# Splitting a mixture-of-experts layer's weights five chunks ahead instead of three

## The chip, the cores and the metric

The kernel runs on one core of a Trainium2 chip. The metric is the device time in microseconds of one execution. Before the change the median of 3 runs is 1571.48 us (1569.36 to 1572.67).

## The reference

The reference computes one decoder layer on 512 tokens of width 1024, in float32: an RMS norm with a shift and scale from a conditioning vector, an input projection, retention and differential attention side by side, an output projection, and then a feed-forward part with 32 experts, of which each token uses 4. A final RMS norm closes it. Cut to what matters here:

```python
logits = xt @ w_router + b_router
top_v, top_i = lax.top_k(logits, 4)          # 4 of 32 experts for each token
gate = softmax(top_v)
# for each expert e and its tokens xb:
hid = xb @ w1[e] + b1[e]                     # w1[e]: 1024 x 2048
y = swiglu_clamped(hid) @ w2[e] + b2[e]      # w2[e]: 1024 x 1024
out[token] += gate * y
```

## The kernel before

All 32 experts are run one after the other, each on up to 128 of its tokens. Almost all weights of the program are those of the experts: for each expert w1 comes in 8 chunks of 128 x 2048 numbers and w2 in 4 chunks of the same size, 1 MB each. That makes 12 chunks for an expert and 384 in all.

The products are made in float32 precision out of a faster format (fp32r) that keeps fewer bits. Each operand is split into a high half, which is its rounded value, and a low half, which is the rest. Three products are added: high x high (L521), high x low of the weights (L522), and low of the tokens x high (L523). A chunk of weights is therefore split first: ACT makes the high half (L481), and DVE subtracts it from the raw chunk in place (L484); POOL does L484 for a few chunks around the first expert. One chunk is 12 products on PE: 4 each of L521, L522 and L523.

Weights live in 48 pages of 4 KB for each partition, and one chunk fills two pages. A raw chunk takes one pair of pages, a split chunk two pairs, because its low half stands where the raw chunk was. `Whole(n)` (a kind of `Conv`) is the reserve of split chunks: `run` splits on until `ahead` = n chunks are held, counting the one that PE is using. `Stream.pump` issues the transfers of the next raw chunks on SP's queue as soon as pages are free, but leaves 2 pages for each split that is still to be made:

```python
kept = self.keep
if self.conv is not None:
    kept += 2 * (self.conv.ahead - len(self.conv.made))
if self.mem.n_free - n < kept or self.mem.find(n) is None:
    return
```

When PE has used up a chunk, `Whole.done` frees its four pages, the next raw chunk is sent for, and the next split is made. In the expert part 12 pages or so are held by other buffers, so that 18 pairs are left for weights: 3 split chunks and 12 raw ones before. From `e == E - LAST - 1` on, `st.keep = 12` holds 12 pages back for the sums at the end.

The loop over the experts runs w1 of expert e (16 calls of `w1_unit`) and then w2 of expert e - 1 (8 calls of `w2_unit`), so that what lies between the two products has time. Around them stand small steps on all engines: `index` finds the tokens of an expert two ahead (L1064 to L1080; the gather is an indirect DMA on POOL), `turn` and `turn_hidden` transpose tokens on PE (L1092, L1099) and split them on ACT and DVE (L1087, L1088), `w1_start` puts the bias into PSUM (L1109), `swiglu` runs on ACT and DVE (L1127 to L1129), and `result` scales the output (L1205, ACT) and adds it into a table in DRAM (L1206, POOL). In the tail the table is read back and added (L1176, L1177, DVE), and the last two experts are put in by products (L1160).

The source is not the order in which the instructions run. A scheduling layer takes the program when it is built and fixes, for each engine, the order in which its instructions stand, by its own estimates of how long things take. On the chip each engine then works through its list from the top, and an instruction that waits holds up all behind it. So a number such as the depth of the reserve moves instructions in all lists.

Of the kernel before, what the change touches and what calls it, by code (L numbers as in the profile page):

```python
# [191 lines left out]
def decoder_layer(ctx, tc, t, out):  # L192
# [793 lines left out]
                      OH[:, i, :].bitcast(F32), start=(i == 0 and k % 4 == 0), stop=(i == NT - 1 and k % 4 == 3))  # L986
            tc.keep_in_program_order(ins)

    cm = Whole(3)
    u1, u2 = {}, {}  # L990
    for e in range(E + 1):
        if e < E:
# [487 lines left out]
```

## Time and profile before

| | us |
|---|---|
| median of 3 runs | 1571.48 |
| profiled execution | 1568.56 |
| its span | 1566.6 |
| PE busy | 1468.6 |
| DVE busy | 1319.4 |
| ACT busy | 1002.4 |
| POOL busy | 164.1 |

The expert part fills the span from about 320 us on. The shares are averages over the whole span. A PE that is shown as busy is not a PE at its peak, because the ends of its instructions are modelled and overlap by some 0.17 us; what a stretch costs is better read from the distance between instructions that come once for each expert. All times below are from the start of the span.

### The profile page before, as it was taken

The numbers are of one execution on the slowest core, as the hardware profiler recorded it, in microseconds if no ns is written. First come the engines' busy times: TensorE is split into PE (matmuls) and PEld (weight loads), VectorE is DVE, ScalarE is ACT, GpSimd is POOL, SyncE is SP. The second block draws the span as 40 slices with busy tenths as digits, with TensorE's granted clock in tenths as the row PEclk, the third lists the DMA queues.
The fourth block names the chain that finished last, engine by engine and source line by source line (L and its number), as shares of the span: only waits on it lengthen the run. The fifth ranks groups of instructions, "written<-read, shape, count | busy, mean of one in ns | idle before, by whom it ended". The sixth has DMA issues, their size and how long they took to land.

```text
span 1566.6 us, 18635 instructions
## 1 busy us (share of the span) xinstructions
PE 1468.6 (94%) x6837; PEld 1193.5 (76%) x6837; DVE 1319.4 (84%) x1407; ACT 1002.4 (64%) x917; POOL 164.1 (10%) x92
## 2 busy tenths in 40 slices
PE   3999999788999999999999999999999999999976
PEld 3787678666888888888887777777777777887754
DVE  6868767977999899899988888888888888888886
ACT  4435434465777777777767666666666666776753
POOL 0000000422100110000011000000000001110001
PEclk8999999988999999999999999999999999999978
DMA  9871473658999999999999999999999999997862
GB/s 371 319 271 37 153 269 138 252 201 320 354 359 367 364 355 362 367 368 365 371 360 349 347 341 346 340 346 345 345 342 335 343 351 345 353 344 259 310 228 98
DMA packets 88812, 485.19 MB, mean 310 GB/s; under 512 B 12433, under 2 KB 18996, under 8 KB 39182
## 3 DMA queue, kind: packets, MB, share of 16 engines
q1 hardware_dynamic: 75792, 453.54, 77.2%
q0 software_dynamic: 9360, 18.05, 4.7%
q10 hardware_dynamic: 3566, 12.37, 2.1%
q8 instruction: 56, 0.92, 0.2%
q14 instruction: 38, 0.31, 0.1%
HBM read 475.82 MB, written 25.44 MB: 320 GB/s over the span
## 4 chain that ended last, share of the span: by engine, by line
PE 74%; DVE 12%; DMA 7%; ACT 5%; issue 2%; POOL 0%; ACTq 0%; DVEq 0%; SPq 0%; POOLq 0%
PE ps L522 22%; PE ps L523 22%; PE ps L521 20%; DVE part L484 6%; DMA page<-in_w_dram 5%; ACT part L481 4%; PE ps L1099 2%; PE ps L1109 1%; PE ps L1092 1%; DVE page L372 1%; PE ps L708 1%; PE ps L788 1%; PE ps L797 1%; PE ps L733 1%; DMA page<-x_dram 0%
## 5 line engine op out<-in xcount | busy, mean ns | idle before, releaser
L484 DVE TENSOR_TENSOR part<-page,part 128x2048 fp32r<-128x2048 f32 x380 | 861.4, 2290 | 106.2 <-ACT part L481 104.2
L481 ACT ACTIVATE part<-page 128x2048 fp32r<-128x2048 f32 x384 | 726.2, 1914 | 144.5 <-PE ps L522 133.3
L522 PE MATMUL ps<-part,part 128*128 128x512 f32 x1792 | 718.9, 401 | 33.1 <-DVE part L484 28.2
L523 PE MATMUL ps<-part,part 128*128 128x512 f32 x1792 | 706.3, 394 | 3.4 <-DVE part L1088 3.4
L521 PE MATMUL ps<-part,part 128*128 128x512 f32 x1792 | 634.0, 397 | 5.7 <-ACT part L616 3.2
L522 PEld LDWEIGHTS ps<-part,part 128*128 128x128 f32 x1792 | 339.6, 189 | 118.1 <-DVE part L484 45.7
L521 PEld LDWEIGHTS ps<-part,part 128*128 128x128 f32 x1792 | 339.5, 190 | 80.8 <-issue 3.7
L523 PEld LDWEIGHTS ps<-part,part 128*128 128x128 f32 x1792 | 339.4, 189 | 73.5 <-DVE part L1088 4.1
L1087 ACT ACTIVATE part<-ps 128x512 fp32r<-128x512 f32 x128 | 73.8, 598 | 139.7 <-PE ps L522 64.8
L1206 POOL DMA_INDIRECT y_dram<-page,idx x30 | 74.8, 2492 | 771.1 <-ACT page L1205 735.7
L1088 DVE TENSOR_TENSOR part<-ps,part 128x512 fp32r<-128x512 f32 x128 | 86.4, 686 | 33.3 <-ACT part L1087 33.2
L1127 ACT ACTIVATE page<-ps 128x512 f32<-128x512 f32 x64 | 37.4, 586 | 74.0 <-PE ps L523 74.0
L1080 POOL DMA_INDIRECT page<-h_dram,idx x31 | 46.4, 1497 | 246.1 <-DVE gs L1071 232.8
L1128 DVE TENSOR_SCALAR page<-ps 128x512 f32<-128x512 f32 x64 | 43.8, 687 | 10.8 <-ACT page L1127 10.8
L447 ACT ACTIVATE part<-page 128x1024 fp32r<-128x1024 f32 x32 | 33.5, 1055 | 27.3 <-DMA page<-in_w_in_dram 9.0
L1129 DVE SCALAR_TENSOR_TENSOR page<-page,page 128x512 f32<-128x512 f32 x64 | 46.7, 733 | 0.0
L450 DVE TENSOR_TENSOR part<-page,part 128x1024 fp32r<-128x1024 f32 x32 | 38.7, 1221 | 9.2 <-ACT part L447 8.9
L1099 PEld LDWEIGHTS ps<-ident,page 128*128 128x128 f32 x256 | 40.1, 203 | 7.1 <-issue 2.5
L420 DVE SCALAR_TENSOR_TENSOR page<-page,sc,page 128x1024 f32<-128x1024 f32 x32 | 40.9, 1280 | 4.6 <-DMA page<-in_w_ada_dram 4.1
L1109 PE MATMUL ps<-part,selr 128*128 128x512 f32 x128 | 39.4, 403 | 4.7 <-DVE page L1128 3.8
L1099 PE MATMUL ps<-ident,page 128*128 128x128 f32 x256 | 41.8, 284 | 2.1 <-DVE page L1129 2.1
L1092 PE MATMUL ps<-ident,page 128*128 128x128 f32 x248 | 37.4, 272 | 0.0
(219 smaller groups left out, 774.2 us busy)
## 6 DMA issues: line engine op xcount, KB each, us to landing
page<-in_w_dram SPq DMA_DIRECT2D x384, 1024.0 KB
page<-in_w_ada_dram SPq DMA_DIRECT2D x22, 1024.0 KB
page<-in_w_in_dram SPq DMA_DIRECT2D x12, 1024.0 KB
page<-in_w_out_dram SPq DMA_DIRECT2D x4, 1024.0 KB
page<-in_x_dram SPq DMA_DIRECT2D x4, 512.0 KB
page<-in_w_ada_dram SPq DMA_DIRECT2D x4, 512.0 KB
page<-in_x_dram SPq DMA_DIRECT2D x2, 1024.0 KB
x_dram<-page ACTq DMA_DIRECT2D x4, 512.0 KB
```

The costliest lines, as they stand in the source:

```text
L481: ins = act.activation(h.r, b.ap, AF.Copy)
L484: ins = self.sub.tensor_tensor(b.r, b.ap, h.r.bitcast(F32), op=ALU.subtract)
L521: pe.matmul(o, aH, bH, start=first, stop=False)
L522: pe.matmul(o, aH, bL, start=False, stop=False)
L523: pe.matmul(o, aL, bH, start=False, stop=last)
L1087: act.activation(hb.r[:, cs], bank(b + n), AF.Copy)
L1088: dve.tensor_tensor(lb.r[:, cs], bank(b + n), hb.r[:, cs].bitcast(F32), op=ALU.subtract)
L1092: pe.transpose(bank(4 + k // 4)[:, (k % 4) * P:(k % 4 + 1) * P], src[:, k * P:(k + 1) * P], ident)
L1099: pe.transpose(bank(4 + k // 4)[:, (k % 4) * P:(k % 4 + 1) * P], src[:, k // 2, k % 2, :], ident)
L1109: pe.matmul(bank(n), selr[:, h * E + e:h * E + e + 1].to_broadcast([P, P]), b12.r[:, n % 2 * 512:(n % 2 + 1) * 512], start=True, stop=False)
L1129: dve.scalar_tensor_tensor(sg.ap[:, cs], sg.ap[:, cs], SILU_MAX, ub.ap[:, cs], op0=ALU.min, op1=ALU.mult)
L1206: pool.indirect_dma_start(out=y_dram, out_offset=bass.IndirectOffsetOnAxis(ap=idx[e % 6][:, 1:2], axis=0), in_=yb.ap, in_offset=None, boun ...
```

## The change

One number: the reserve is `Whole(5)` instead of `Whole(3)`.

```diff
-    cm = Whole(3)
+    cm = Whole(5)
     u1, u2 = {}, {}
     for e in range(E + 1):
         if e < E:
```

Five chunks may be split at a time, the one in use included. They take 10 of the 18 pairs of pages instead of 6, so 8 raw chunks lie ahead of them instead of 12, and the ring of both is 13 chunks instead of 15. No instruction is added or left out, but the scheduling layer sets many of them elsewhere. Three places show it. In the listings L484 reads the raw chunk (page_2_...) and the high half (second part_2_...) and writes the low half; numbers are those of buffers.

The first place is POOL's list around the first expert, from the subtraction for chunk 0 to the fourth token gather (L1080), before:

```order
L484 TENSOR_TENSOR part_2_2166<-page_2_87,part_2_352 128x2048
L967 TENSOR_TENSOR page_1_1831<-page_1_1831,page_1_243 128x512 x2
L1080 DMA page_1_782<-h_dram,idx_2236 128x1024
L484 TENSOR_TENSOR part_2_2257<-page_2_95,part_2_316 128x2048
L1080 DMA page_1_2156<-h_dram,idx_2237 128x1024
L484 TENSOR_TENSOR part_2_2426<-page_2_246,part_2_592 128x2048
L484 TENSOR_TENSOR part_2_1704<-page_2_116,part_2_247 128x2048
L1080 DMA page_1_782<-h_dram,idx_2238 128x1024
```

and the same stretch of POOL's list after:

```order
L484 TENSOR_TENSOR part_2_2164<-page_2_87,part_2_1760 128x2048
L967 TENSOR_TENSOR page_1_1831<-page_1_1831,page_1_243 128x512 x2
L1080 DMA page_1_782<-h_dram,idx_2234 128x1024
L484 TENSOR_TENSOR part_2_2255<-page_2_95,part_2_2253 128x2048
L484 TENSOR_TENSOR part_2_2259<-page_2_1641,part_2_2257 128x2048
L484 TENSOR_TENSOR part_2_2262<-page_2_1643,part_2_316 128x2048
L1080 DMA page_1_2156<-h_dram,idx_2235 128x1024
L484 TENSOR_TENSOR part_2_460<-page_2_101,part_2_592 128x2048
L484 TENSOR_TENSOR part_2_2253<-page_2_284,part_2_247 128x2048
L1080 DMA page_1_782<-h_dram,idx_2236 128x1024
```

POOL splits six chunks instead of four: the two more are chunks 2 and 3 of the first expert, ahead of the second gather.

The second place is ACT's list behind the tenth L1205 (`result(9)`), where an expert of the middle begins, before:

```order
L1205 ACTIVATE page_1_2699<-ps,gate_2244 128x1024
L481 ACTIVATE part_2_2426<-page_2_97 128x2048
L1087 ACTIVATE part_1_2516<-ps 128x512 x2
L481 ACTIVATE part_2_1704<-page_2_270 128x2048
L481 ACTIVATE part_2_460<-page_2_99 128x2048
L481 ACTIVATE part_2_1760<-page_2_105 128x2048
L481 ACTIVATE part_2_528<-page_2_87 128x2048
L481 ACTIVATE part_2_316<-page_2_95 128x2048
L481 ACTIVATE part_2_352<-page_2_1641 128x2048
L1127 ACTIVATE page_1_140<-ps 128x512
L481 ACTIVATE part_2_2166<-page_2_79 128x2048
```

and after:

```order
L1205 ACTIVATE page_1_2703<-ps,gate_2242 128x1024
L481 ACTIVATE part_2_592<-page_2_101 128x2048
L1087 ACTIVATE part_1_2520<-ps 128x512 x2
L481 ACTIVATE part_2_247<-page_2_284 128x2048
L481 ACTIVATE part_2_267<-page_2_79 128x2048
L1087 ACTIVATE part_1_2248<-ps 128x512
L481 ACTIVATE part_2_2390<-page_2_99 128x2048
L481 ACTIVATE part_2_1704<-page_2_97 128x2048
L481 ACTIVATE part_2_460<-page_2_87 128x2048
L481 ACTIVATE part_2_2253<-page_2_2427 128x2048
L1127 ACTIVATE page_1_93<-ps 128x512
L1087 ACTIVATE part_1_2248<-ps 128x512
```

An L1087 for the next expert's tokens, which stood behind the two L1127, now stands among the L481 ahead of them. Before has this arrangement too, in later experts.

The third place is DVE's list in the tail, from the second L1176 (the sums that were read back) to the last SwiGLU (L1128), before:

```order
L1176 TENSOR_TENSOR page_1_242<-page_1_242,page_1_83 128x1024
L484 TENSOR_TENSOR part_2_2166<-page_2_87,part_2_460 128x2048
L1176 TENSOR_TENSOR page_1_67<-page_1_67,page_1_83 128x1024
L484 TENSOR_TENSOR part_2_2257<-page_2_95,part_2_592 128x2048
L1176 TENSOR_TENSOR page_1_9352<-page_1_9352,page_1_83 128x1024
L484 TENSOR_TENSOR part_2_2306<-page_2_1641,part_2_1760 128x2048
L1177 TENSOR_TENSOR page_1_9342<-page_1_9342,page_1_9344 128x1024
L1177 TENSOR_TENSOR page_1_9346<-page_1_9346,page_1_242 128x1024
L1128 TENSOR_SCALAR page_1_2444<-ps 128x512 x2
```

and after:

```order
L1176 TENSOR_TENSOR page_1_9352<-page_1_9352,page_1_83 128x1024
L484 TENSOR_TENSOR part_2_2259<-page_2_1641,part_2_1704 128x2048
L1177 TENSOR_TENSOR page_1_9346<-page_1_9346,page_1_9348 128x1024
L1177 TENSOR_TENSOR page_1_9350<-page_1_9350,page_1_9352 128x1024
L1176 TENSOR_TENSOR page_1_67<-page_1_67,page_1_83 128x1024
L1176 TENSOR_TENSOR page_1_9358<-page_1_9358,page_1_83 128x1024
L1177 TENSOR_TENSOR page_1_9354<-page_1_9354,page_1_67 128x1024
L1177 TENSOR_TENSOR page_1_69<-page_1_69,page_1_9358 128x1024
L484 TENSOR_TENSOR part_2_1723<-page_2_2427,part_2_460 128x2048
L484 TENSOR_TENSOR part_2_2314<-page_2_1647,part_2_2253 128x2048
L484 TENSOR_TENSOR part_2_2255<-page_2_95,part_2_2257 128x2048
L1128 TENSOR_SCALAR page_1_2448<-ps 128x512 x2
```

The adds stand together ahead of three splits instead of between the splits, and one chunk more is split ahead of the SwiGLU: 7 chunks are still to be split there instead of 8.

## Rows read from the trace of the kernel before

**Rows 1.** The page, part 1: busy time of each engine, share of the span and count of instructions.

```profile
PE 1468.6 (94%) x6837; PEld 1193.5 (76%) x6837; DVE 1319.4 (84%) x1407; ACT 1002.4 (64%) x917; POOL 164.1 (10%) x92
```

**Rows 2.** Busy time in two stretches of the expert part: stretch, its length, busy time and count for PE, PEld, DVE, ACT and POOL, then the granted clock of PE, the share of the DMA engines and GB/s.

```profile
400.00:760.00 360.00, 360.00 (x1681) 300.04 (x1680) 327.26 (x241) 271.63 (x191) 38.39 (x20) 1.00 0.97 364
830.00:1330.00 500.00, 483.92 (x2206) 391.45 (x2205) 430.70 (x320) 345.66 (x250) 52.73 (x27) 1.00 0.95 344
```

**Rows 3.** The timeline of ACT, of which only L1205 stands here: results 0, 10, 11, 12 and 29. Columns: start, length, engine and line, what it writes and reads, and the idle time before it with what ended it.

```profile
400.18 1.09 ACT L1205 ACTIVATE page<-ps,gate 128x1024 f32<-128x1024 f32 x1
...
760.29 1.09 ACT L1205 ACTIVATE page<-ps,gate 128x1024 f32<-128x1024 f32 x1
794.98 1.12 ACT L1205 ACTIVATE page<-ps,gate 128x1024 f32<-128x1024 f32 x1 [1.06 <-PE ps L523]
833.48 1.12 ACT L1205 ACTIVATE page<-ps,gate 128x1024 f32<-128x1024 f32 x1 [1.20 <-PE ps L523]
...
1481.44 1.12 ACT L1205 ACTIVATE page<-ps,gate 128x1024 f32<-128x1024 f32 x1
```

**Rows 4.** Who waited for whom: four rows of one late expert (1062.68 to 1100.84 us), then one of the stretch from 375 to 800 us. Columns: us in total, times, longest.

```profile
ACT part L1087 <- PE ps L522: 3.9, 1, 3.9
...
ACT page L1127 <- PE ps L523: 3.2, 1, 3.2
PEld ps L522 <- DVE part L484: 2.2, 3, 1.4
...
ACT part L481 <- PE ps L522: 1.4, 2, 0.7
...
ACT part L481 <- PE ps L522: 86.6, 120, 1.2
```

**Rows 5.** The timelines of ACT, DVE and PE in that late expert, in this order.

```profile
1081.17 1.92 ACT L481 ACTIVATE part<-page 128x2048 fp32r<-128x2048 f32 x1 [0.69 <-PE ps L522]
1086.28 0.60 ACT L1127 ACTIVATE page<-ps 128x512 f32<-128x512 f32 x1 [3.19 <-PE ps L523]
...
1087.45 1.91 ACT L481 ACTIVATE part<-page 128x2048 fp32r<-128x2048 f32 x1
...
1094.12 1.92 ACT L481 ACTIVATE part<-page 128x2048 fp32r<-128x2048 f32 x1 [0.68 <-PE ps L522]
...
1079.98 6.68 DVE L484 TENSOR_TENSOR part<-page,part 128x2048 fp32r<-128x2048 f32 x3
...
1089.39 2.29 DVE L484 TENSOR_TENSOR part<-page,part 128x2048 fp32r<-128x2048 f32 x1 [1.11 <-ACT part L481]
...
1095.60 4.49 DVE L484 TENSOR_TENSOR part<-page,part 128x2048 fp32r<-128x2048 f32 x2
...
1091.74 0.49 PE L522 MATMUL ps<-part,part 128*128 128x512 f32 x1 [0.95 <-DVE part L484]
```

**Rows 6.** The timelines of POOL, DVE and PE in the first expert, in this order: chunk 1's subtraction on POOL, DVE's next rows, and four rows of PE (the first L522 of chunk 1, the next chunk's L521, and the first and last of the 12 products of chunk 4).

```profile
324.06 4.54 POOL L484 TENSOR_TENSOR part<-page,part 128x2048 fp32r<-128x2048 f32 x1
...
323.75 5.41 DVE L1064 TENSOR_TENSOR OH<-cst,posm 128x512 fp32r<-128x512 f32 x1
...
329.21 6.68 DVE L484 TENSOR_TENSOR part<-page,part 128x2048 fp32r<-128x2048 f32 x3
...
328.66 0.50 PE L522 MATMUL ps<-part,part 128*128 128x512 f32 x1 [3.84 <-POOL part L484]
...
331.65 1.60 PE L521 MATMUL ps<-part,part 128*128 128x512 f32 x4
...
338.89 0.39 PE L521 MATMUL ps<-part,part 128*128 128x512 f32 x1
...
341.43 0.39 PE L523 MATMUL ps<-part,part 128*128 128x512 f32 x1
```

**Rows 7.** Transfers of weights. First the waits of ACT for them; then a stretch of 3 us with columns as in rows 2; then two pieces of the chain of waits (start, length, what); then SP's timeline from 215 us to 1081.3 us, and the count of ACT's L481 in a stretch that ends at 1087.40 us.

```profile
ACT part L481 <- DMA page<-in_w_dram: 4.0, 5, 0.8
...
1131.00:1134.00 3.00, 3.00 (x16) 2.55 (x15) 3.00 (x4) 2.34 (x2) 0.00 (x0) 1.00 0.58 194
...
1081.39 6.01 DMA page<-in_w_dram
1087.45 1.92 ACT part L481
...
222.07 856.06 SPq L134 DMA_DIRECT2D page<-in_w_dram  x255
...
300.00:1087.40 787.40, 466.32 (x245) 0.99 0.93 345
```

**Rows 8.** The timelines of DVE and PE in the tail, in this order.

```profile
1496.24 1.23 DVE L1176 TENSOR_TENSOR page<-page,page 128x1024 f32<-128x1024 f32 x1 [6.42 <-DMA page<-y_dram]
...
1507.39 2.29 DVE L484 TENSOR_TENSOR part<-page,part 128x2048 fp32r<-128x2048 f32 x1
...
1499.72 0.79 PE L522 MATMUL ps<-part,part 128*128 128x512 f32 x1 [6.02 <-DVE part L484]
...
1513.95 1.95 PE L1099 MATMUL ps<-ident,page 128*128 128x128 f32 x8 [2.10 <-DVE page L1129]
1518.39 1.22 PE L521 MATMUL ps<-part,part 128*128 128x512 f32 x2 [2.48 <-ACT part L481]
1520.71 0.80 PE L522 MATMUL ps<-part,part 128*128 128x512 f32 x1 [1.10 <-DVE part L484]
```

## Prediction

> **What bounds the kernel now.** The engine table comes first: TensorE (PE) is busy for 94% of the span, DVE for 84%, ACT for 64% [rows 1]. An average hides where the loss is, so the second view is the busy time in two long stretches [rows 2]. From 400 to 760 us PE is busy for all 360.00 us; from 830 to 1330 us for only 483.92 of 500, at the same granted clock of 1.00.
>
> The third view dates the change. L1205 takes the result of one expert out of PSUM, so its starts are the beat of the loop [rows 3]. Result 0 leaves at 400.18 and result 10 at 760.29: (760.29 - 400.18) / 10 = 36.01 us for each expert. Result 11 leaves at 794.98 and result 29 at 1481.44: (1481.44 - 794.98) / 18 = 38.14 us. So 18 experts are slower by 2.13 us each, 38.3 us in all, which is the most that a deeper reserve could win in the loop.
>
> The fourth view says what is waited for in one late expert [rows 4]. PE waits 2.2 us for L484, the low half of a split, in three pieces. ACT waits for PE 3.9 us at an L1087 and 3.2 at L1127, and only 1.4 us at L481 for pages that PE frees. Before 800 us it is the other way round: there L481 waits 120 times for PE to free pages, 86.6 us in all.
>
> **Why a depth of five helps little.** The listing of the order decides this, not the diff. The order is fixed when the program is built. I counted how many L481 stand ahead of each L1205 and took off the chunks that PE has used by then (12 for each expert, and 20 at the first result): that is the lead of the splits. Before, it is 3 up to result 10 and 2 from result 11 on. After, it is 5 up to result 5, then 4 and 3, and 2 from result 8 on. With a lead of 2 the products soon stand in what I call the late pattern: the four L521 of the next chunk are pulled ahead of its L522 and L523, and ACT's L1087 stand among the L481. In the order of before this pattern begins behind result 11, just where the beat changes from 36.01 to 38.14. In the order of after it begins behind result 8. From result 16 until the tail PE, ACT and DVE have the same instructions in the same places in both, chunk for chunk; only buffer numbers differ.
>
> So in the late experts the fourth and fifth splits have pages but do not stand earlier in any queue. What is left is that an L481 need not wait for a page. In the late expert of [rows 5], the L481 at 1081.17 waits 0.69 us for one and ends at 1083.09; its L484 is the third of three that begin at 1079.98. Each but the last takes (6.68 - 2.29) / 2 = 2.2 us there, so it starts at 1084.4, 1.3 us later. The L481 at 1094.12 ends at 1096.04; its L484 starts at 1095.60 + 2.2 = 1097.8. Neither page wait is on the path. PE's long wait ends at 1091.74. It is for the L484 of 1089.39, which waited 1.11 us for the L481 of 1087.45, which stands behind the L1127 of 1086.28, which had waited 3.19 us for PE's last product of w1. The order makes this wait, and five splits deep it is the same.
>
> **The sum**, on the profiled execution: 1568.56 us, 1566.6 of it the span.
>
> Middle: three more experts (those that end with results 9, 10 and 11) run in the late pattern: 3 x 2.13 = +6.4 us. Experts with a lead of 5 gain nothing, since PE is busy throughout at a lead of 3 [rows 2]. The expert in which before goes over took 833.48 - 794.98 = 38.50 us [rows 3], only 0.4 above a late one, and after has one like it. Low end 0, if the pages do pay in the three; high end 9, if each costs 3 us.
>
> Start: POOL makes the low halves of chunks 0 to 3 instead of 0 and 1. One takes 4.5 us on POOL, 2.2 us on DVE [rows 6]. Before, PE waits 3.84 us for chunk 1 until 328.66 and then not again for a while, as DVE does chunks 2 to 4 in 6.68 us from 329.21. After, POOL goes on: chunk 2 is ready at 328.6 + 4.5 = 333.1, chunk 3 at 337.6. PE ends chunk 1's products at 331.65 and wants chunk 2's low half at 332.0 (1.1 us late); it runs 11 products at 0.23 (chunk 4's 12 begin from 338.89 to 341.43) and one more, and wants chunk 3's at 335.9 (1.7 late), chunk 4's at 340.4. DVE's L1064 took 5.41 us and ended 0.6 us behind POOL's split; if it is held until 337.6 now, chunk 4 is ready at 337.6 + 0.6 + 2.2 = 340.4, in time. Chunk 4's products end at 342.9, against 341.43 + 0.23 = 341.7 before, and one more pair of L1196 (0.5 us) is still to come: +1.7 us. Bounds: 0, if PE's slow clock behind its first wait hides it, and +7, by the rival on the port.
>
> The row shows a DVE instruction with two SBUF inputs held until POOL's one ended. The Trainium skill ("SBUF — State Buffer", section "SBUF: two separate sides") calls this an exclusive lock, kept for the whole instruction by whoever starts first. By that, DVE could take it between two POOL splits, and the sum would be the rival's below; no row here shows who gets it between two.
>
> The last two POOL splits of the first expert stay, as chunks 11 and 12 instead of 9 and 10, and PE's waits behind them are not for L484: 0.
>
> Transfers: the ring of chunks, split and raw, falls from 15 to 13. ACT waited for weights 5 times, 4.0 us in all [rows 7]. The queues run dry now and then: 194 GB/s at a share of 0.58 in one stretch of 3 us [rows 7]. 8 raw chunks are 8 x 3 = 24 us ahead, against 6.01 us for the transfer that SP issued at 1081.39 [rows 7]. So 0.
>
> Tail: DVE waits 6.42 us for the gathered sums until 1496.24, PE therefore 6.02 us until 1499.72, and later 2.10, 2.48 and 1.10 us around the last SwiGLU [rows 8]. After, the last w1 split stands behind eight adds and three other splits: 1496.24 + 8 x 1.14 + 4 x 2.2 = 1514.1, instead of 1507.39 + 2.29 = 1509.7. But two chunks of w2 (24 products of 0.23 us, 5.5 us) now stand ahead of the L1099 and run beside the chain that PE waits out for 5.7 us, and some of the 6.02 is bridged by the deeper splits. That is 4.4 lost against some 6.5 won: -2 us, with -7 (most waits gone) and +5 (nothing won) as ends.
>
> Sum: 6.4 + 1.7 + 0 - 2 = +6.1 us. The profiled execution is 2.9 us below the median of the runs, 1571.48, so I add the sum to the median: 1577.6 us, 0.4% slower. A change below 0.2% (3.1 us) can't be told from none here.
>
> **Rivals.**
> The depth does pay in the late experts and the 2.13 us go. For it: each PE wait there is for L484, the longest 1.4 us [rows 4], and two chunks are 5.4 us. Against it: the same places in the queues. From result 8 on 21 experts would run at 36.0 instead of 38.14, which wins the whole 38 us of before: 1571.5 - 38 + 2 - 2, about 1533 us. It decides from the first expert behind result 8. Chance 0.08.
> Middle and tail cancel: the going over is mild and the tail wins its 7 us: 6.4 + 2 - 7, about 1573 us, no change. For it: 11.7 us of PE waits to win from in the tail. Against it: the last w1 split comes later. Chance 0.19.
> POOL and DVE take turns at the port in the start: chunk 2 is ready at 328.6 + 0.6 + 2.2 + 4.5 = 335.9 and chunk 3 at 342.6, so PE waits 3.9 + 3.9 us instead of 1.1 + 1.7. That is 5 us more: about 1583 us. For it: DVE was held, not refused, by one POOL split; against it: no row between two. Chance 0.10.
> Weights come late: the chain of waits puts a weight transfer that ends at 1087.40 right ahead of the L481 of 1087.45 [rows 7]. If landing were the limit, a ring of 13 instead of 15 would stretch the late beat to 38.14 x 15 / 13 = 44.0: 18 x 5.9 = 106 us more, about 1680 us. Against it: by then SP had issued 255 transfers and ACT begun 245 splits [rows 7], so the one issued at 1081.39 is for a chunk ten further on. Chance 0.05.
> My forecast: 0.58.
>
> **Range and chances.** The forecast's own terms span 1569 to 1588; I give 1568 to 1588, which leaves out the first and the last rival. Slower by over 0.2%: the forecast nearly whole (0.54), the port, the weights and a little of the cancelling case, 0.71. Faster: the first rival and a part of the cancelling case, 0.11. The same: 0.18.
>
> **What would show it.** Starts of L1205 36.0 us apart up to result 8 and 38.1 from there on. Six L484 on POOL, with PE waiting for the third and fourth between 332 and 341 us. In a late expert PE still waits 2.2 us for L484, while ACT's waits at L481 are gone. If the late beat falls to 36, the main step is wrong and the order is not what makes the wait; if the early beat rises above 36.2, it is the weights.

## The result and the profile after

The changed kernel takes 1585.43 us (median of 4 runs, 1581.74 to 1586.82), the kernel before 1570.72 us beside it: a ratio of 1.0089 (95% interval 1.0068 to 1.0110), so 14.0 us slower by the ratio. The forecast was 6.1 us slower. The profiled execution took 1585.85 us, its span 1584.0.

The starts of L1205 and the first split on POOL divide both spans into four stretches that add up:

| us | before | after | difference | forecast |
|---|---|---|---|---|
| span's start to the first split on POOL | 303.09 | 306.28 | +3.2 | 0 |
| first split to result 0 | 97.09 | 100.89 | +3.8 | +1.7 |
| result 0 to result 29 | 1081.26 | 1086.56 | +5.3 | +6.4 |
| result 29 to the end | 85.16 | 90.27 | +5.1 | -2 |

Up to the first split PE, DVE, ACT and POOL have the same instructions in the same order in both kernels. In the eleven other executions profiled below that also split first on POOL, that stretch takes 303.3 to 305.4 us at any depth, so I take the 3.2 us for scatter of this one execution. The other three add up to 14.2 us, against 14.7 between the medians (14.0 by the ratio).

First the page of the changed kernel, part 1, and three groups of its part 5: busy time, mean ns, idle time before the group and what ended most of it.

```profile
PE 1473.3 (93%) x6837; PEld 1195.5 (75%) x6837; DVE 1323.9 (84%) x1405; ACT 993.9 (63%) x917; POOL 171.3 (11%) x94
...
L481 ACT ACTIVATE part<-page 128x2048 fp32r<-128x2048 f32 x384 | 718.8, 1912 | 80.9 <-PE ps L522 70.7
L522 PE MATMUL ps<-part,part 128*128 128x512 f32 x1792 | 721.6, 403 | 49.2 <-DVE part L484 41.9
...
L1127 ACT ACTIVATE page<-ps 128x512 f32<-128x512 f32 x64 | 37.6, 589 | 118.8 <-PE ps L523 118.8
```

The same two groups of L481 and L522 on the page of the kernel before:

```profile
L481 ACT ACTIVATE part<-page 128x2048 fp32r<-128x2048 f32 x384 | 726.2, 1914 | 144.5 <-PE ps L522 133.3
L522 PE MATMUL ps<-part,part 128*128 128x512 f32 x1792 | 718.9, 401 | 33.1 <-DVE part L484 28.2
```

Against [rows 1] the engines are as busy as before. What changed is what they wait for: ACT's high halves wait less for pages that PE frees (70.7 us; before, 133.3), ACT waits longer for PE at L1127 (118.8 us; before, 74.0), and PE waits more for the low halves (41.9 us; before, 28.2).

The beat, from ACT's timeline: results 0, 7, 8, 9, 10 and 29.

```profile
407.17 1.10 ACT L1205 ACTIVATE page<-ps,gate 128x1024 f32<-128x1024 f32 x1
...
657.61 1.12 ACT L1205 ACTIVATE page<-ps,gate 128x1024 f32<-128x1024 f32 x1 [2.56 <-PE ps L523]
693.65 1.12 ACT L1205 ACTIVATE page<-ps,gate 128x1024 f32<-128x1024 f32 x1 [2.61 <-PE ps L523]
731.13 1.12 ACT L1205 ACTIVATE page<-ps,gate 128x1024 f32<-128x1024 f32 x1 [3.12 <-PE ps L523]
769.52 1.12 ACT L1205 ACTIVATE page<-ps,gate 128x1024 f32<-128x1024 f32 x1
...
1493.73 1.12 ACT L1205 ACTIVATE page<-ps,gate 128x1024 f32<-128x1024 f32 x1
```

Result 8 comes 36.0 us behind result 7, result 9 comes 37.5 later, result 10 38.4 later, and from there the beat is (1493.73 - 769.52) / 19 = 38.12 us. In [rows 3] this begins three results later.

Who waited for whom in a late expert of the changed kernel (1074.97 to 1113.13 us); columns as in [rows 4].

```profile
ACT page L1127 <- PE ps L523: 4.0, 1, 4.0
ACT part L1087 <- PE ps L522: 3.9, 1, 3.9
...
PEld ps L522 <- DVE part L484: 2.2, 3, 1.4
```

PE's wait for L484 is the same 2.2 us as in [rows 4]. No L481 waits for a page any more, and that won nothing.

The start, in the order POOL, DVE, PE, ACT; the rows answer to [rows 6]. Behind them stand two rows of the kernel before: PE's wait at L1109 and ACT's table load.

```profile
327.06 13.57 POOL L484 TENSOR_TENSOR part<-page,part 128x2048 fp32r<-128x2048 f32 x3
...
326.74 14.45 DVE L1064 TENSOR_TENSOR OH<-cst,posm 128x512 fp32r<-128x512 f32 x1
...
341.25 15.49 DVE L484 TENSOR_TENSOR part<-page,part 128x2048 fp32r<-128x2048 f32 x7
...
336.16 0.50 PE L522 MATMUL ps<-part,part 128*128 128x512 f32 x1 [0.66 <-POOL part L484]
340.69 0.50 PE L522 MATMUL ps<-part,part 128*128 128x512 f32 x1 [1.50 <-POOL part L484]
362.10 2.08 PE L1109 MATMUL ps<-part,selr 128*128 128x512 f32 x4 [4.85 <-DVE page L1128]
...
357.52 1.90 ACT L481 ACTIVATE part<-page 128x2048 fp32r<-128x2048 f32 x1
359.43 1.28 ACT L1127 ACT_TABLE_LOAD   x1
```

```profile
355.41 1.33 PE L1109 MATMUL ps<-part,selr 128*128 128x512 f32 x4 [3.75 <-DVE page L1128]
...
352.74 1.28 ACT L1127 ACT_TABLE_LOAD   x1
```

DVE's L1064 (0.68 us elsewhere) is held through three splits of POOL. PE waits 0.66 + 1.50 us for the third and fourth chunk (chunks 2 and 3). Then it waits 4.85 us at expert 1's first L1109, where it waited 3.75 before: ACT still makes a high half until 359.42, and the table load for L1127 stands behind it, 2.2 us after PE's last row ahead of the wait (before, 1.1).

The tail, in the order DVE, PE, POOL, SP, to be read against [rows 8]. L1173 loads the sums from y_dram; SP's row counts what it sends until POOL asks. Behind it stand the rows of POOL and SP in the kernel before.

```profile
1513.47 1.23 DVE L1176 TENSOR_TENSOR page<-page,page 128x1024 f32<-128x1024 f32 x1 [11.35 <-DMA page<-y_dram]
...
1526.96 6.69 DVE L484 TENSOR_TENSOR part<-page,part 128x2048 fp32r<-128x2048 f32 x3
...
1516.95 0.79 PE L522 MATMUL ps<-part,part 128*128 128x512 f32 x1 [10.95 <-DVE part L484]
...
1529.30 0.80 PE L522 MATMUL ps<-part,part 128*128 128x512 f32 x1 [5.19 <-DVE part L484]
...
1540.97 0.50 PE L522 MATMUL ps<-part,part 128*128 128x512 f32 x1 [1.59 <-DVE part L484]
...
1505.33 0.60 POOL L1173 DMA_DIRECT2D page<-y_dram  x1 [7.75 <-PE ps L523]
...
1496.45 9.00 SPq L134 DMA_DIRECT2D page<-in_w_dram  x4
```

```profile
1490.45 2.22 POOL L1173 DMA_DIRECT2D page<-y_dram  x4 [5.17 <-PE ps L523]
...
1490.11 0.33 SPq L134 DMA_DIRECT2D page<-in_w_dram  x1
```

DVE reaches the first add of the sums (L1176) and waits 11.35 us for rows of y_dram; the split that PE needs stands right behind that add. Before, the wait was 6.42 us [rows 8]. Ahead of POOL's first load SP has sent four transfers of weights behind result 29; before, it was one.

### The profile page after: what moved, and what is told of

It is laid out like the page before. It is cut to its first block, busy times and chain, and to the rows that moved or that the text cites. A ratio compares the mean times of both kernels' runs of the same rounds, so it can differ in the third digit from the quotient of the medians.

```text
span 1584.0 us, 18643 instructions
## 1 busy us (share of the span) xinstructions
PE 1473.3 (93%) x6837; PEld 1195.5 (75%) x6837; DVE 1323.9 (84%) x1405; ACT 993.9 (63%) x917; POOL 171.3 (11%) x94
## 4 chain that ended last, share of the span: by engine, by line
PE 58%; DVE 8%; ACT 5%; DMA 5%; issue 2%; POOL 1%; ACTq 0%; DVEq 0%; POOLq 0%
PE ps L522 19%; PE ps L523 18%; PE ps L521 16%; DVE part L484 6%; ACT part L481 5%; DMA page<-in_w_dram 3%; PE ps L1099 2%; PE ps L1092 1%; PE ps L1109 1%; DMA y_dram<-page,idx 1%; POOL part L484 1%; DMA page<-y_dram 1%; DVE page L1129 0%; DVE page L1368 0%; DMA page<-x_dram 0%
## 5 line engine op out<-in xcount | busy, mean ns | idle before, releaser
L484 DVE TENSOR_TENSOR part<-page,part 128x2048 fp32r<-128x2048 f32 x378 | 855.3, 2287 | 98.8 <-ACT part L481 96.6
L481 ACT ACTIVATE part<-page 128x2048 fp32r<-128x2048 f32 x384 | 718.8, 1912 | 80.9 <-PE ps L522 70.7
L522 PE MATMUL ps<-part,part 128*128 128x512 f32 x1792 | 721.6, 403 | 49.2 <-DVE part L484 41.9
L521 PE MATMUL ps<-part,part 128*128 128x512 f32 x1792 | 623.3, 396 | 3.3 <-ACT part L616 3.2
L522 PEld LDWEIGHTS ps<-part,part 128*128 128x128 f32 x1792 | 339.6, 190 | 137.4 <-DVE part L484 61.7
L521 PEld LDWEIGHTS ps<-part,part 128*128 128x128 f32 x1792 | 338.9, 189 | 78.4 <-issue 3.7
L1087 ACT ACTIVATE part<-ps 128x512 fp32r<-128x512 f32 x128 | 74.1, 598 | 170.2 <-PE ps L1099 81.4
L1127 ACT ACTIVATE page<-ps 128x512 f32<-128x512 f32 x64 | 37.6, 589 | 118.8 <-PE ps L523 118.8
L1080 POOL DMA_INDIRECT page<-h_dram,idx x31 | 47.6, 1534 | 282.7 <-DVE gs L1071 270.5
L1128 DVE TENSOR_SCALAR page<-ps 128x512 f32<-128x512 f32 x64 | 43.8, 687 | 22.0 <-ACT page L1127 21.9
L1109 PE MATMUL ps<-part,selr 128*128 128x512 f32 x128 | 40.8, 411 | 5.8 <-DVE page L1128 4.8
L1205 ACT ACTIVATE page<-ps,gate 128x1024 f32<-128x1024 f32 x30 | 33.5, 1116 | 15.6 <-PE ps L523 15.6
L1099 PE MATMUL ps<-ident,page 128*128 128x128 f32 x256 | 41.8, 279 | 0.0
```

Source lines behind the costliest of these rows:

```text
L481: ins = act.activation(h.r, b.ap, AF.Copy)
L484: ins = self.sub.tensor_tensor(b.r, b.ap, h.r.bitcast(F32), op=ALU.subtract)
L521: pe.matmul(o, aH, bH, start=first, stop=False)
L522: pe.matmul(o, aH, bL, start=False, stop=False)
L1080: pool.indirect_dma_start(out=Xg[e % 2].ap, out_offset=None, in_=h2_dram, in_offset=bass.IndirectOffsetOnAxis(ap=idx[e % 6][:, 0:1], axis= ...
L1087: act.activation(hb.r[:, cs], bank(b + n), AF.Copy)
```

## Experiments

Ratios are to the kernel before, run beside each on the same chip; stretches are those of the table above. An experiment is told by its label (e1 and so on); the diffs show only the lines that matter.

**Undoing the two ends.** The changed kernel with three splits ahead at the start (e1), in the tail (e2), or both (e3).

```diff
-            cm.sub = dve                    # e1: Whole(3), and behind expert 0's products
+            cm.sub, cm.ahead = dve, 5
-                st.keep = 12                # e2: Whole(5), and at e == E - LAST - 1
+                st.keep, cm.ahead = 12, 3
```

> Three splits ahead until expert 0's products are issued, five from there on: the start of the expert part stands in the order of the kernel before (one split on POOL, then a gather, then two), the middle and the tail in the order of the changed kernel. Theory (the 17.4 us of span that the change added are 3.8 in the start, 5.3 in the middle, 5.1 in the tail and 3.2 ahead of the expert part, where the instructions stand alike and the times of two executions merely differ): 3.8 us less than the changed kernel, about 1581.6 us, and the DVE's L1064 beside POOL's splits back from 14.45 us to about 5.4. Rival (the start's 3.8 us is the same scatter between executions): 1585, with L1064 at 5.4 all the same and the first result no earlier against the first split than in the changed kernel.

> Five splits ahead, but three from the last experts on: the start and the middle stand as in the changed kernel, the tail of DVE in the order of the kernel before (a split between each two of the sums L1176). Theory (the tail's 5.1 us come from L1176 standing ahead of the splits that PE waits for, while its own rows of y_dram land late, so that L522 waits 10.95 and 5.19 us): 5 us less than the changed kernel, about 1580 us, and from result 29 to the end about 85 us. Rival (the tail's length is set by when the weights' transfers leave y_dram's loads the DMA engines, whatever the order on DVE): about 1585 us, 90 us from result 29 to the end, and the wait of L1176 still above 10 us.

> Both of these edits: five splits ahead between expert 0 and the last experts alone. Theory: the middle's term is left by itself, 5.3 us over the kernel before, about 1576 us (1574 to 1578); the late beat of 38.1 us begins behind result 8. Rival (the 3.2 us ahead of the expert part belong to the change as well): about 1579 us, and the first split on POOL again some 3 us later than the kernel before's 303.09.

e1: 1581.13 us, ratio 1.0070 (1.0055 to 1.0085); from first split to result 0 96.7 us, L1064 back to 5.40 us. e2: 1579.2 us, 1.0065 (1.0050 to 1.0079); start 101.1, tail 85.9. e3: 1577.8 us, 1.0048 (1.0034 to 1.0062); start 96.9, tail 86.2, first split at 303.38. In all three the middle takes 1086.2 to 1086.6 us. Each stretch follows its own edit and no other: the start's 3.8 to 4 us and some 4.3 us of the tail are shown as the depth's work, and what is left is the middle and about 1 us of the tail. The other profiles below bear this out with some scatter: where POOL splits first, starts three deep take 94.4 to 99.5 us, most of them near 97, and the one more that is five deep (e6) 100.9; the rows of y_dram are there 14.7 to 15.8 us behind result 29 in all tails three deep (12.2 in e9, which gives pages back there), and 19.1 to 21.2 us in those five deep. The medians agree with that within their scatter: e3 stands 7.2 us over the kernel before, where the stretches give 6. e2's tail, in the order DVE, PE, POOL, SP:

```profile
1506.32 1.23 DVE L1176 TENSOR_TENSOR page<-page,page 128x1024 f32<-128x1024 f32 x1 [6.72 <-DMA page<-y_dram]
...
1509.81 0.80 PE L522 MATMUL ps<-part,part 128*128 128x512 f32 x1 [6.33 <-DVE part L484]
...
1500.33 0.60 POOL L1173 DMA_DIRECT2D page<-y_dram  x1 [5.27 <-PE ps L523]
...
1499.88 0.33 SPq L134 DMA_DIRECT2D page<-in_w_dram  x1
```

Counted from result 29 (1491.22 here, 1493.73 in the changed kernel), POOL asks for the sums after 9.1 us instead of 11.6, and they land 6.0 us later instead of 8.1. In the changed kernel SP sends for weights 2.7 us behind result 29, here 8.7 us behind it. The edit moves the page that the sums wait for, the weights sent ahead of them and the order on DVE together; how the 5 us divide among these is not shown.

**Is it the order?** The instructions of the loop are held in the order in which the kernel names them, for experts 1 to 29. `kp` calls `keep_in_program_order` where its engine is in a set that is filled ahead of each `w1_start(e)` (that line is left out here). The engines that are not held still get a new order from the build. e5 holds PE, ACT and DVE with three splits ahead, e6 the same with five, e7 PE alone, e8 ACT alone.

```diff
-            ins = act.activation(h.r, b.ap, AF.Copy)                # L481; so too L1087, L1127, L1205
+            ins = kp('act', act.activation(h.r, b.ap, AF.Copy))
-            ins = self.sub.tensor_tensor(b.r, b.ap, ...)            # L484; so too L1088, L1128, L1129
+            ins = kp('dve', self.sub.tensor_tensor(b.r, b.ap, ...))
-        pe.matmul(o, aH, bH, start=first, stop=False)               # L521; so too L522, L523
+        kp('pe', pe.matmul(o, aH, bH, start=first, stop=False))
```

> Three splits ahead as in the kernel before; from expert 1 to the last two the products (L521 to L523), the splits (L481, L484), L1087, L1088, L1127 to L1129 and L1205 are each held in the order in which the kernel names them, so that the late order does not arise. Theory (the order, not the supply of weights or pages, makes the late beat): 36.0 us between results to the end instead of 38.1 behind result 11, some 18 times 2.13 us less, about 1534 us. Rival (the late beat is what the transfers of weights allow once the reserve of the start is used up): 38.1 us or more stays, 1571 us or slower, and ACT's L481 wait for weights from about result 11 on.

> The same order held, with five splits ahead. Theory (in this loop the depth is worth nothing of its own; the order was all): 36.0 us between results throughout, as with three, and over the kernel with three only the start's 3.8 us and what the tail adds (up to 5): 1534 to 1543 us. Rival (with the order out of the way a deeper reserve of splits does help): faster than the kernel with three in the held order by more than 3 us.

> Three splits ahead; only the products L521 to L523 are held in the order in which the kernel names them, so that the four L521 of the next chunk are not pulled ahead; ACT and DVE keep the late order. Theory (ACT makes the wait: its L481 stands behind an L1127 or L1087 that waits for PE): the late beat stays at 38.1 us or gets longer, since PE has no L521 to run while it waits, 1571 to 1590 us. Rival (the L521 pulled ahead are the cause): 36.0 us, about 1534 us.

> Three splits ahead; only ACT is held (L481, L1087, L1127, L1205), PE and DVE are left to the order that the build makes of it. Theory (ACT makes the wait): the late beat falls to near 36.0 us, 1534 to 1545 us. Rival (PE's and DVE's order make it): 38.1 us stays, 1571 us.

| | us | ratio | beat, results 14 to 25 (us) | middle (us) |
|---|---|---|---|---|
| e5, all, three ahead | 1540.5 | 0.9798 (0.9775 to 0.9820) | 36.1 | 1049.5 |
| e6, all, five ahead | 1539.3 | 0.9801 (0.9781 to 0.9822) | 36.0 | 1043.3 |
| e7, PE, three ahead | 1547.2 | 0.9844 (0.9828 to 0.9861) | 36.8 | 1058.5 |
| e8, ACT, three ahead | 1537.4 | 0.9792 (0.9766 to 0.9817) | 36.1 | 1048.7 |

The late beat is made by the order: with the same instructions and the order held, it is 36.0 or 36.1 us. With ACT held, PE is busy for all of the stretch in which it had been busy for 483.92 us [rows 2], and the weights keep up at 363 GB/s; e8's windows (columns as in [rows 2]), the waits of one of its late experts (1059.0 to 1095.1 us), and a row of PE from it:

```profile
830.00:1330.00 500.00, 500.00 (x2329) 414.27 (x2328) 453.57 (x330) 368.64 (x261) 81.41 (x28) 1.00 0.97 363
...
ACT part L481 <- PE ps L522: 7.7, 9, 1.3
...
1060.86 1.07 PE L521 MATMUL ps<-part,part 128*128 128x512 f32 x4
```

PE's waits for L484 are gone, and L481 waits for pages again, as it did before 800 us. PE's list in e8 still has four L521 of the next chunk pulled ahead, five times in an expert (six before), so that this half of the late pattern costs next to nothing where ACT's order is held. DVE's list is another than before in e8, so the share of ACT's order alone is not isolated; that holding it is enough is shown.

e7 fits neither expectation: 38.1 - 36.8 = 1.3 of the 2.1 us go. It does not leave ACT's late order as it was, as its expectation had it. No four L521 stand together any more, and ACT's list is new too: between the two L1127 of an expert it has one L481, where before it had an L1087 and an L481. The lead of the splits still falls to 2 behind result 11, and ACT still waits for PE at L1127, but PE waits less for L484 (0.8 us, against 2.2 in [rows 4]). Two rows of e7's waits in a late expert (1062.81 to 1099.58 us):

```profile
ACT page L1127 <- PE ps L523: 3.5, 1, 3.5
...
PEld ps L522 <- DVE part L484: 0.8, 1, 0.8
```

So e7 says only that the price of a lead of 2 depends on the rest of the order. As I read it, PE waits for a split that stands on ACT behind an L1127, and that L1127 waits for PE; no run here tests this ring by itself.

Of the depth, e6 against e5 says that it wins 0.1 us for an expert and 4 us in the last four results (36.0 and 36.1; 142.9 and 146.8 us). The start (100.9 against 99.1) and the tail (88.7 against 86.1) give it back, e5's start being 2 us longer than most three deep: the medians differ by 1 us, too little to tell.

**What makes the order turn?** Three splits ahead, with fewer chunks lying ahead. e4 keeps four pages free from the first expert on. e9 keeps eight free for two experts, and from expert 2 on takes four pairs of pages out of use until the tail, where it gives them back.

```diff
-    cm.pinned, cm.sub = False, dve
+    cm.pinned, cm.sub, st.keep = False, dve, 4      # e4, and no more; in e9 8, and the lines below
...
+            hold, st.keep = ([Buf(mem, 2) for _ in range(4)], 0) if e == 2 else (hold if e > 2 else [], st.keep)
-                st.keep = 12
+                st.keep, _ = 12, [b.free() for b in hold]
```

> Three splits ahead as in the kernel before, but four pages kept free from the first expert on, so that two raw chunks fewer lie ahead; nothing else is edited. Theory (it is the raw chunks lying ahead, not the splits, that set where the order turns into the late one): the turn comes one to two experts earlier, some 2 to 4 us over the kernel before, 1573 to 1575 us. Rival (the number of splits ahead makes the late order or its price): the same as the kernel before, 1571 us, with the beat of 36.0 us up to result 11.

> Three splits ahead as in the kernel before, but from expert 2 to 29 four pairs of pages are taken and not used, so that 8 raw chunks lie ahead instead of 12 and no split can stand earlier than before (the lead counted in the order is 3, as in the kernel before, where four free pages alone had made it 4). Theory (it is the chunks lying ahead, raw and split, that set where the order turns into the late one): the late order begins some four experts earlier, about four times 2.1 us more, less up to 3 us in the last two experts where the pages are given back: 1576 to 1580 us, with beats of 38 us from result 7 or 8 on. Rival (the depth of the splits makes the late order): the beat of 36.0 us holds up to result 11 and the time is the kernel before's, 1571 us.

e4: 1571.01 us, 1.0004 (0.9996 to 1.0013), by the time the rival's. Its beat turns one result earlier all the same, and its middle is 2.8 us longer. It doesn't separate the two: in its order the free pages let a fourth split stand earlier, so that it is four splits deep in effect (the lead counted in its list is 4 up to result 7 and 2 from result 9). e9 mends that: 1575.83 us, 1.0035 (1.0024 to 1.0046), the lower edge of the theory's range; its middle is 8.1 us longer (1.6 of it between results 0 and 1, ahead of the late order), its start 2.7 and its tail 1.9 us shorter. Results 7 to 10 of e9:

```profile
651.83 1.12 ACT L1205 ACTIVATE page<-ps,gate 128x1024 f32<-128x1024 f32 x1 [1.03 <-PE ps L523]
690.54 1.12 ACT L1205 ACTIVATE page<-ps,gate 128x1024 f32<-128x1024 f32 x1 [1.54 <-PE ps L523]
729.06 1.12 ACT L1205 ACTIVATE page<-ps,gate 128x1024 f32<-128x1024 f32 x1
767.20 1.12 ACT L1205 ACTIVATE page<-ps,gate 128x1024 f32<-128x1024 f32 x1
```

With a lead of three, as before, and 11 chunks lying ahead instead of 15, the beat of 38 us begins with result 8 instead of 12. The depth is not needed for the late order; fewer chunks ahead are enough. How much of the changed kernel's early turn is the ring's is not shown: with a ring of 13 like it, e4 comes to a lead of 2 one result later (9 instead of 8), and its middle is longer by 2.8 us instead of 5.3.

**The start.** The first low halves on DVE instead of POOL, five ahead (e10) and three ahead (e13).

```diff
-    cm.sub = pool
+    cm.sub = dve
     cm.make()
```

> Five splits ahead as in the changed kernel, but the low halves of the first chunks are made on DVE instead of POOL; the rest is edited nowhere. Theory (the start's 3.8 us are three splits back to back on POOL at 4.5 us each, with DVE's L1064 kept waiting through all of them): with 2.2 us a split on DVE the start falls by at least those 3.8 us, from first split to first result some 95 us or less, and no L1064 takes over 1 us; 1581 us or less. Rival (DVE is the engine that is short at the start, and POOL only looks slow): the start is as long as in the changed kernel or longer, 1585 us or more.

> Three splits ahead as in the kernel before, with the first chunks' low halves on DVE. Theory (POOL's splits are the whole cost of the start, the depth has none of its own): from first split to first result 86 us, as five deep with DVE, so some 11 us less than the kernel before, about 1560 us. Rival (the depth pays at the start once the splits are short): a start of 90 us or more, 1564 us or more.

e10: 1572.66 us, 1.0003 (0.9992 to 1.0014), 12.8 us less than the changed kernel: from the first L481 to result 0 it takes 90.9 us, where the changed kernel takes 102.9 and the kernel before 99.1. DVE in e10:

```profile
325.44 0.68 DVE L1064 TENSOR_TENSOR OH<-cst,posm 128x512 fp32r<-128x512 f32 x1
326.17 2.28 DVE L484 TENSOR_TENSOR part<-page,part 128x2048 fp32r<-128x2048 f32 x1
328.50 2.28 DVE L484 TENSOR_TENSOR part<-page,part 128x2048 fp32r<-128x2048 f32 x1
330.83 8.88 DVE L484 TENSOR_TENSOR part<-page,part 128x2048 fp32r<-128x2048 f32 x4
```

No L1064 is held there, and PE waits for no split. About half of the gain over the kernel before stands ahead of the products: PE's second L1109 of this start comes 10.6 us behind the first L481, where it came 14.7 before. In the kernel before, DVE's L899, an add of one number for each partition that takes 0.15 us in e10, was held beside POOL's first split, and PE waited 5.14 us for the chain that follows:

```profile
303.18 4.49 DVE L899 TENSOR_TENSOR n2s<-n2s 128x1 f32<-128x1 f32 x1
```

e13: 1564.09 us, 0.9949 (0.9930 to 0.9968), and 93.5 us for that stretch, 2.7 more than e10. By the time that is the rival's (1564 or more). But e14 below, which has e13's order up to 362 us, takes 90.6 us, and 2.1 of the 2.9 us between these two pass before PE's second L1109, where the two runs differ in PE's granted clock (e13, then e14; columns as in [rows 2]):

```profile
305.00:310.00 5.00, 5.00 (x26) 5.00 (x25) 4.12 (x13) 1.83 (x3) 2.16 (x1) 0.50 0.83 338
...
305.00:310.00 5.00, 5.00 (x39) 4.99 (x39) 4.55 (x17) 1.93 (x3) 1.64 (x1) 0.83 0.89 360
```

In e13 the clock is at the lower of its two levels (1.2 GHz) for all of these 5 us, in e14 for a part of them; PE had been busy for 4.06 and 3.67 of the 5 us before. Counted from PE's second L1109 on, five deep (e10) takes 80.3 us and three deep 81.3 (e13) and 80.5 (e14). So it is for the larger part the clock that put e13 on its rival's side, and whether the depth wins anything (0.2 to 1 us by these counts) at a start without POOL stays open. The 11 us that both expectations took off were too many: they were counted from the first low half, which begins 4.8 us behind the first L481 on DVE and 2.0 behind it on POOL. From the first L481 it is 99.1 - 90.9 = 8.2 us.

**Put together.** Three ahead at both ends, five between, the order held: ACT (e11), PE, ACT and DVE (e12), and e12 with the first splits on DVE (e14).

> ACT alone held in the order of the kernel (L481, L1087, L1127, L1205), with five splits ahead between expert 0 and the last experts, three at both ends. Theory (the terms add up): the start and the tail of the kernel before (97 and 86 us), the middle of the five deep kernel in the held order (1043 us), about 1531 us, so 6 us less than with three splits ahead and ACT held. Rival (those 6 us came with DVE and PE held as well): 1537 us.

> The same with the products on PE and the splits and halves on DVE held too. Theory: 97 + 1043 + 86 us behind a first split at about 303, 1531 us. Rival (in the tail the held order costs what it wins, since DVE's sums L1176 stand in another order there): 1535 us or more.

> All that was found put together: the first low halves on DVE, three ahead in expert 0 and five from there on, the order of PE, ACT and DVE held up to the last two experts, three ahead in the tail. Theory (start, middle and tail are independent terms): 11 us less than the same kernel with POOL's splits (1533.5), about 1522 us. Rival (what the start wins is given back later in expert 0 or the middle): 1530 us or more.

e11: 1534.92 us, 0.9764 (0.9743 to 0.9784). e12: 1533.53 us, 0.9770 (0.9749 to 0.9791). e14: 1527.57 us, 0.9721 (0.9702 to 0.9740). The middle is 1045.0, 1043.8 and 1043.8 us. e11 and e12 come within some 4 us of the 1531 us that the terms add up to, and are not told apart. Against e12, e14 wins 6.0 us between the medians (7.7 by the ratios, as the two ran on different chips), of the 8.2 just counted. It is 44.7 us (2.8%) faster than the kernel before in the runs beside it (1572.29); its windows, to be read against [rows 2]:

```profile
400.00:760.00 360.00, 360.00 (x1679) 300.01 (x1678) 329.14 (x241) 268.87 (x190) 56.67 (x20) 1.00 0.97 365
830.00:1330.00 500.00, 500.00 (x2332) 416.68 (x2331) 451.21 (x332) 367.69 (x264) 78.19 (x28) 1.00 0.98 365
```

## Why the prediction was right and wrong

**The side and the main mechanism were right, the sum was less than half.** The order decides, the late pattern comes three experts earlier, and in a late expert the extra pages win nothing: beats, waits and e5, e6 and e8 show each of these. The tail is the term that failed worst, by 7.1 us, then the start, by 2.1; the middle was 1.1 too much. The rival by which the depth pays in the late experts is out: with the late order left, the beat was 38.1. The rival by which weights come late is out as well: at 36.0 us an expert they come at 363 GB/s.

**Middle, +6.4, measured +5.3.** Right but for the going over, which cost 1 us less than before, for the most part in one expert: the first late beat is 37.5 us, where it was 38.5 (result 12 in [rows 3]).

**Start, +1.7, measured +3.8.** The moments on POOL, DVE and PE were right: set back by the 3.0 us by which chunk 1 is later, the third and fourth chunk were ready and L1064 came free within 0.1 us of what was worked out. PE's two waits, 0.66 + 1.50 us, are near the 1.1 + 1.7 forecast. Two steps failed. I let the slow end of chunk 1's products cover part of these waits, which it didn't: from the first split to PE's last row ahead of the wait at L1109 the changed kernel takes 2.4 us more, not 1.7. And behind the first five chunks the change was to cost nothing: ACT, with 13 high halves to make by then instead of 11, comes later to the table load of expert 0's SwiGLU, and PE's wait there grew by 1.10 us. The two make 3.5 us of the 3.8. The rival of the port gave a time (1583) near the one measured, by a mechanism that didn't occur: POOL and DVE did not take turns. By the rule of the Trainium skill ("SBUF — State Buffer", section "SBUF: two separate sides") whoever starts first keeps the port for that instruction. It doesn't say who gets it between two. The trace does: DVE's L1064 ended 0.6 us behind POOL's third split (341.19 and 340.63). Who started first cannot be read from these rows: L1064's row begins 0.32 us ahead of POOL's first split, and it was L1064 that was held; spans on POOL are rough.

**Tail, -2, measured +5.1.** The largest miss, and the step that failed is plain: I worked from 1496.24 us, the moment at which y_dram's rows landed before, as if the change left it where it was. They landed 19.7 us behind result 29 instead of 14.8 [rows 8]. The deeper splits were to bridge a part of PE's 6.02 us; PE ran out of products 12.3 us behind result 29 in both kernels, since the next L484 stands behind the first L1176 in both. So nothing was bridged and the wait grew to 10.95 us. The listing showed the order, and I took the landing of a transfer from a trace in which it was asked for earlier and one transfer of weights had been sent ahead of it, not four. The other two steps were nearer: the adds that now stand together cost PE 5.19 us where 4.4 were forecast, and around the last SwiGLU PE waits 1.59 and 0.23 us where it waited 5.7, so 3.9 us were won of the 6.5. With the 4.9 us of the longer first wait these come to 6.2 us, of which 1.1 was made up elsewhere. The end of +5 stood for "nothing won"; that the term came out there is luck, because the late landing was in none of its ends.

**The range** (1568 to 1588) held the time, by the luck of the tail's upper end. The ends of the three terms add up to 1564.5 to 1592.5 us, not to the 1569 to 1588 that I called their span.

## What to carry to other kernels

Where a scheduler fixes the order at build time, a deeper reserve is first a change of order. Read the order that it leaves, and ask of every wait whether the waiting instruction could stand elsewhere: here holding one engine's order won 2.1%, while more depth alone lost 0.9%. Before a term is costed at the end of a kernel, ask, of each transfer that the end waits for, when it is issued and what is sent ahead of it; its landing time in the old trace is no constant.

## What the runs showed of the hardware

DVE's L1064, an instruction with two inputs in SBUF (0.68 us alone), took 5.41 us beside one split on POOL and 14.45 us beside three back to back: DVE was not let in between them. A far smaller instruction was held as well: L899, with one number for each partition, took 4.49 us beside a split on POOL and 0.15 us in e10, where no split runs beside it. The same split takes 4.5 us on POOL and 2.2 us on DVE in a row, so each of the two moved to POOL held L1064 some 4.5 us longer to take 2.2 us off DVE.

POOL loads the sums from y_dram in four transfers of 512 KB. DVE could begin the first add 5.8 and 6.0 us after POOL's issue where SP had sent one transfer of weights ahead of it, 0.3 and 0.5 us earlier (the kernel before, e2), and 8.1 us where it had sent four, the first of them 8.9 us earlier (the changed kernel). The DMA engines were at a share of 1.00 to 1.01 from 1503 to 1513 us there. Early weights alone do not make the loads slow: in e10 SP had sent four as well, but POOL asked only 3.9 us behind the last of them, held by the landing of the last result's scatter into y_dram, and the loads were there after 5.9 us.

```profile
1495.61 0.60 POOL L1173 DMA_DIRECT2D page<-y_dram  x1 [11.43 <-DMA y_dram<-page,idx]
```
